# The first feed-forward network by seven products over all tokens, with some weight remainders made by adding DMAs

## The chip, the cores and the metric

The kernel runs on one core of a Trainium2 chip. The metric is the device time of one execution in microseconds (us); less is better. The core's engines work in parallel, each through its own list of instructions in order, and wait for one another by semaphores: PE (TensorE, matrix products; PEld loads its weights), DVE (VectorE), ACT (ScalarE), POOL (GpSimd) and SP (SyncE, which here only issues DMAs). Matrix products write to PSUM, a small memory of eight banks; everything else lies in SBUF.

## The reference

Two layers work on 512 latent tokens (`x`) and 256 context tokens (`ctx`) of width 1024. Each layer has adaLN-modulated norms, an attention block and a SwiGLU feed-forward network (FFN) with 2816 hidden columns. In layer 0 the FFN is computed for both kinds of token, in layer 1 for the latent tokens only.

```python
FFN_HIDDEN = (8 * D_MODEL + 3 * 256 - 1) // (3 * 256) * 256      # 2816
def swiglu(h, w1, w3, w2):
    return (jax.nn.silu(h @ w1) * (h @ w3)) @ w2

for layer in range(DEPTH):                                       # DEPTH = 2
    ctx_out = layer < DEPTH - 1
    ...
    h_x = modulate(rmsnorm(x, norm_g[layer, 1]), mod_x[3], mod_x[4])
    x = x + mod_x[5] * swiglu(h_x, ffn_w1[layer], ffn_w3[layer], ffn_w2[layer])
    if ctx_out:
        ctx = ctx + mod_c[2] * o_c
        h_c = modulate(rmsnorm(ctx, norm_g[layer, 1]), mod_c[3], mod_c[4])
        ctx = ctx + mod_c[5] * swiglu(h_c, ffn_w1[layer], ffn_w3[layer], ffn_w2[layer])
return rmsnorm(x, final_g)
```

## The kernel before

**Numbers.** Every operand of a product is kept as two fp32r parts: `hi`, a rounded copy, and `lo`, what is left of it. A product is three matmuls, hi·hi, hi·lo and lo·hi (`mm3`, L187, L188, L189). `split` (L182, L183) makes the parts: ACT copies to `hi`, DVE subtracts `hi` from the source to make `lo`. For weights loaded by the stream of weights `S`, the same work stands in L154 (ACT) and L155 (DVE). A token operand `h` lies feature-major, in eight tiles of 128 features: `hx[k]` holds both parts of 512 latent tokens, `hc[k]` of 256 context tokens. The residual streams are `xr` and `cr` (`res` in the profile).

**FFN of layer 0** (`ffn`, called once with layer 0; 493 to 1056 us of the profiled execution). The hidden columns are 22 tiles of 128. For each tile, `mm13` computes `w1` and then `w3`: 8 feature tiles of three matmuls of 512 columns for `x` and of 256 columns for the context, into one PSUM tile of two banks. ACT takes the silu of the first (L1058), DVE multiplies by the second (L1065), and `split` makes `g`. Tiles come in groups of two. The down product of a group (`do2`, `mm3` again) is cut into 16 pieces, one for each of 8 output tiles and each kind of token; a piece ends with DVE adding the gated product to the residual (L1125). The pieces of a group are strewn among the products of the next group. PSUM has two pools of two such tiles, used in the order 0, 0, 1, 1.

**What else runs there.** `filler` gives DVE the modulation rows of the remaining adaLN parts: each of the 56 loads of `in_ada_wT_dram` (512 KB) is read twice, by L249 and L250. Two buffers take these loads; a new load is asked for when one has been read. The context's norm (`norm_c`) runs within the first tile: its sum over features is the matmul L289 with a matrix of ones. The order on each engine is set by the scheduler of the language when the kernel is built; it is fixed in the program.

**FFN of layer 1** works by seven products already (Strassen's scheme in Winograd's form): the feature dimension, the hidden columns of a pair of tiles and the tokens are each cut into two halves, and seven products of quarter size (L1486, L1487, L1488; 256 columns, four feature tiles each) take the place of eight. DVE makes the sums of the weights (L448, L449, L451, L452) and puts the products together (L1504, L1505, L1506, L1510, L1512).

Of the kernel before, what the change touches and what calls it, by code (L numbers as in the profile page):

```python
# [15 lines left out]
P = 128  # L16
# [16 lines left out]
def f32(ap):  # L33
    return ap.bitcast(F32)
# [3 lines left out]
def tile_trunk(  # L38
# [145 lines left out]

    def mm3(ps, wh, wl, xh, xl, n=KT):
        for k in range(n):
            nc.tensor.matmul(ps, wh(k), xh(k), start=k == 0, stop=False)  # L187
            nc.tensor.matmul(ps, wh(k), xl(k), start=False, stop=False)  # L188
            end = nc.tensor.matmul(ps, wl(k), xh(k), start=False, stop=k == n - 1)  # L189
        return end  # L190
# [130 lines left out]
    hx, hc = [None] * KT, [None] * KT  # L321

    def h_tiles(*which):
        for k in range(KT):
            if "x" in which:
                hx[k] = hpool.tile([P, 2, NX], F32R, tag=f"hx{k}", name="hx")
            if "c" in which:
                hc[k] = hpool.tile([P, 2, NC], F32R, tag=f"hc{k}", name="hc")
# [77 lines left out]
    groups = [list(range(g, min(g + GRP, HT))) for g in range(0, HT, GRP)]  # L406
    groups = groups[:-2] + [groups[-2], groups[-1]]
    NG = len(groups)

    groups2 = groups[:-2] + [groups[-2] + groups[-1]]  # L410

    def ffn_weights(l):


        def add2(g):
            for j in groups2[g]:
                S.add(w2[l, j * P : (j + 1) * P, :], "w2")

        for g in range(NG):
            for j in groups[g]:  # L420
                for w in (w1, w3):
                    S.add(w[l, j])

                    if 0 < g < NG - 1 and (j, w is w1) == ((groups[g][0], True) if g > 1 else (groups[g][-1], False)):
                        add2(g - 1)
        add2(NG - 2)

# [62 lines left out]

    ada1 = [(l, s_, k) for l, s_ in [(0, 5)] + [(1, z) for z in range(6)] for k in range(KT)]
    ada1_at = [ada1[max(0, 3 * n - 3) : min(3 * n, KT)] if n < 4 else [] for n in range(2 * NG)]
    for i, z in enumerate(ada1[KT:]):
        ada1_at[4 + i * (2 * NG - 8) // (6 * KT)].append(z)
# [9 lines left out]
    with ExitStack() as st:  # L504
# [36 lines left out]
        with ExitStack() as s0:  # L541
# [4 lines left out]
            h_tiles("x", "c")  # L546
# [390 lines left out]
        for u in range(8):  # L937
# [14 lines left out]
            else:  # L952
# [3 lines left out]
                def prep(m):  # L956
                    def f():
                        if m == 0:
                            h_tiles("x", "c")
# [65 lines left out]
        h_tiles("x")  # L1025
        for k in range(KT):
            h_make(k, hx[k], xr[k], r, 0, 1, 0, nmap)
        ffn_weights(0)
# [4 lines left out]
    def ffn_psum(st):  # L1033

        pools = [st.enter_context(tc.tile_pool(name=f"f_ps{i}", bufs=2, space=PSUM, reuse_waits="tile")) for i in range(2)]
        order = [0, 0, 1, 1]

        def tile_():
            order.append(order.pop(0))
            return pools[order[-1]].tile([P, 1024], F32, tag="f", name="f")  # L1040

        return tile_

    def ffn(l, fp, fps, chunks, first, last, filler=None, between=None, done=None):

        nall = sum(c[3] for c in chunks)
        gt = {}
        evac = [None]  # L1050

        def mm13(ps, w, c):
            wh, wl = (wslice(t) for t in w)
            mm3(ps[:, c[5] : c[5] + c[3]], wh, wl, c[0], c[1])

        def silu_of(j, ps):
            s = fp.tile([P, nall], F32, tag="silu", name="silu", bufs=1)
            act = nc.scalar.activation(s, ps[:, 0:nall], AF.Silu)  # L1058
            if j == HT - 1:
                exp_ln_tables(act)  # L1060
            return s

        def g_of(g, j, ps, s):
            t = fp.tile([P, 2, nall], F32R, tag="g", name="g", bufs=2 * GRP)
            nc.vector.tensor_mul(s, ps[:, 0:nall], s)  # L1065
            end = split(t[:, 0, :], t[:, 1, :], s)
            gt[j] = t
            if g == 0:
                evac[0] = end
            if filler and j == groups[g][0]:  # L1070
                with tc.issue_after(end.ins):
                    filler(2 * g + 1)

        def do13(g, pieces=()):

            pieces = list(pieces)
            n = -(-len(pieces) // (2 * len(groups[g]))) if g > 1 else 0
            if filler and evac[0]:
                with tc.issue_after(evac[0].ins):
                    filler(2 * g)  # L1080
            for j in groups[g]:
                if j == 0:
                    pr = [fps() for _ in range(2)]
                    w = [S.next(), S.next(1)]
                    keep_busy(pr[0], 0 if l else 16, before[0])
                    for ci, c in enumerate(first):
                        for i in range(2):
                            mm13(pr[i], w[i], c)
                            if between and i == 0:
                                between(ci)  # L1090
                else:
                    pr = []
                    for _ in range(2):
                        w = S.next()
                        ps = fps()
                        for c in chunks:
                            mm13(ps, w, c)
# [595 lines left out]
```

## Time and profile before

| what | value |
|---|---|
| time, median of 3 executions | 1674.18 us (1671.73 to 1675.25) |
| the profiled execution's own time | 1676.36 us |
| its span (first to last instruction) | 1674.6 us, 1.8 us less |
| mean granted TensorE clock | 0.99 |
| DVE busy in the FFN of layer 0, 593 to 893 us | 68 to 72 of each 100 us |
| DMA of weights `raw<-in_w_dram` | 132 of 512 KB, 3.8 us from issue to landing |

The page of the profile gives busy times by engine and by group of instructions; a group's line holds the line of the code, the engine, the operation, what is written and read, the shape and count, then the busy time in us and the mean of one in ns, and behind the last bar how long the engine stood idle just before these instructions and what ended the wait. Durations overlap on PE: a matmul starts before the one ahead of it has ended.

### The profile page before, as it was taken

The numbers are of one execution on the slowest core, as the hardware profiler recorded it, in microseconds if no ns is written. First come the engines' busy times: TensorE is split into PE (matmuls) and PEld (weight loads), VectorE is DVE, ScalarE is ACT, GpSimd is POOL, SyncE is SP. The second block draws the span as 40 slices with busy tenths as digits, with TensorE's granted clock in tenths as the row PEclk, the third lists the DMA queues.
The fourth block names the chain that finished last, engine by engine and source line by source line (L and its number), as shares of the span: only waits on it lengthen the run. The fifth ranks groups of instructions, "written<-read, shape, count | busy, mean of one in ns | idle before, by whom it ended". The sixth has DMA issues, their size and how long they took to land.

```text
span 1674.6 us, 26226 instructions
## 1 busy us (share of the span) xinstructions
PE 1609.4 (96%) x10436; PEld 1408.9 (84%) x10436; DVE 1175.9 (70%) x1936; ACT 669.5 (40%) x1235; POOL 233.9 (14%) x270
## 2 busy tenths in 40 slices
PE   5999998999999999999999999999999899999996
PEld 3798987877889888888888888878788798989896
DVE  4758698966578666766766344778665797869685
ACT  4445554556253111112111123456755453524343
POOL 2223113454010000000000000155321000000001
PEclk9999999999999999999999999999999899999998
DMA  9422254644126334534434130221011332323321
GB/s 335 110 55 80 82 161 136 186 133 126 51 76 211 118 113 129 161 112 140 135 117 126 39 101 26 75 80 50 14 39 34 119 126 88 113 90 101 114 76 51
DMA packets 56915, 176.97 MB, mean 106 GB/s; under 512 B 6245, under 2 KB 10501, under 8 KB 56793
## 3 DMA queue, kind: packets, MB, share of 16 engines
q1 hardware_dynamic: 53064, 164.40, 32.2%
q0 software_dynamic: 3152, 10.37, 1.9%
q8 instruction: 82, 1.34, 0.3%
q10 hardware_dynamic: 576, 0.52, 0.1%
q14 instruction: 41, 0.33, 0.1%
HBM read 160.45 MB, written 4.86 MB: 99 GB/s over the span
## 4 chain that ended last, share of the span: by engine, by line
PE 65%; DVE 7%; DMA 3%; ACT 2%; issue 1%; POOL 0%; DVEq 0%; SPq 0%; ACTq 0%; POOLq 0%
PE f L187 10%; PE f L188 10%; PE f L189 10%; PE f L1486 4%; PE f L1488 4%; PE f L1487 4%; PE t L1313 3%; DMA raw<-in_w_dram 2%; PE lin L187 2%; PE lin L189 2%; PE lin L188 2%; DVE wl L155 2%; PE f L1540 2%; PE f L1541 2%; PE t L1299 2%; PE f L1539 2%
## 5 line engine op out<-in xcount | busy, mean ns | idle before, releaser
L154 ACT CAST wh<-raw 128x1024 fp32r<-128x1024 f32 x126 | 131.4, 1049 | 469.2 <-PE f L188 326.1
L155 DVE TENSOR_TENSOR wl<-raw,wh 128x1024 fp32r<-128x1024 f32 x126 | 158.2, 1256 | 81.6 <-ACT wh L154 81.4
L187 PE MATMUL f<-hx,wh 128*128 128x512 f32 (+1 forms) x416 | 161.6, 392 | 6.2 <-DVE res L1125 5.3
L188 PE MATMUL f<-hx,wh 128*128 128x512 f32 (+1 forms) x416 | 160.9, 387 | 0.0
L189 PE MATMUL f<-hx,wl 128*128 128x512 f32 (+1 forms) x416 | 160.5, 386 | 0.0
L188 PE MATMUL f<-g,wh 128*128 128x256 f32 (+1 forms) x416 | 137.1, 330 | 0.0
L189 PE MATMUL f<-g,wl 128*128 128x256 f32 (+1 forms) x416 | 136.0, 328 | 0.0
L187 PE MATMUL f<-g,wh 128*128 128x256 f32 (+1 forms) x416 | 135.5, 330 | 0.0
L187 PE MATMUL lin<-hx,wh 128*128 128x512 f32 x264 | 107.9, 409 | 5.6 <-DVE q L354 2.2
L249 DVE SCALAR_TENSOR_TENSOR junk<-raw,tables 128x1024 bf16<-128x1024 f32 x80 | 98.2, 1228 | 17.7 <-DMA raw<-in_ada_wT_dram 17.1
L188 PE MATMUL lin<-hx,wh 128*128 128x512 f32 x264 | 105.7, 400 | 0.0
L1125 DVE SCALAR_TENSOR_TENSOR res<-f,mod,res 128x512 f32<-128x512 f32 (+1 forms) x160 | 92.3, 613 | 18.6 <-PE f L189 18.3
L188 PE MATMUL f<-hc,wh 128*128 128x256 f32 x368 | 104.2, 285 | 0.9 <-DVE hc L337 0.9
L189 PE MATMUL lin<-hx,wl 128*128 128x512 f32 x264 | 105.0, 398 | 0.0
L189 PE MATMUL f<-hc,wl 128*128 128x256 f32 x368 | 103.6, 283 | 0.0
L187 PE MATMUL f<-hc,wh 128*128 128x256 f32 x368 | 102.7, 283 | 0.3 <-ACT hc L336 0.3
L1065 DVE TENSOR_TENSOR silu<-f,silu 128x768 f32<-128x768 f32 x22 | 21.1, 957 | 114.5 <-PE f L189 114.5
L316 POOL TENSOR_TENSOR ns_a<-ns_a,ns_s 128x256 f32<-128x256 f32 (+1 forms) x20 | 19.7, 984 | 584.8 <-ACT ns_s L312 582.9
L187 PEld LDWEIGHTS f<-hx,wh 128*128 128x128 f32 x416 | 78.6, 190 | 22.8 <-DVE res L1125 7.1
L189 PEld LDWEIGHTS f<-hx,wl 128*128 128x128 f32 x416 | 78.6, 189 | 16.2
L188 PEld LDWEIGHTS f<-hx,wh 128*128 128x128 f32 x416 | 78.9, 190 | 14.1
L187 PEld LDWEIGHTS f<-g,wh 128*128 128x128 f32 x416 | 78.5, 190 | 8.0 <-issue 0.2
(326 smaller groups left out, 4636.4 us busy)
## 6 DMA issues: line engine op xcount, KB each, us to landing
raw<-in_w_dram SPq DMA_DIRECT2D x132, 512.0 KB, 3.8
raw<-in_ada_wT_dram SPq DMA_DIRECT2D x80, 512.0 KB, 3.6
raw<-in_w_ab_dram SPq DMA_DIRECT2D x24, 512.0 KB, 4.1
raw<-in_ada_w_dram SPq DMA_DIRECT2D x16, 512.0 KB, 9.4
k<-k SPq DMA_DIRECT2D x16, 384.0 KB, 5.8
raw<-in_w_c_dram SPq DMA_DIRECT2D x12, 512.0 KB, 3.7
nb<-in_na_bias_dram POOLq DMA_DIRECT2D x16, 256.0 KB, 3.7
raw<-in_wo_ab_dram SPq DMA_DIRECT2D x8, 512.0 KB, 3.7
```

The costliest lines, as they stand in the source:

```text
L154: nc.scalar.copy(hi, raw)
L155: eng.tensor_sub(lo, raw, f32(hi))
L187: nc.tensor.matmul(ps, wh(k), xh(k), start=k == 0, stop=False)
L188: nc.tensor.matmul(ps, wh(k), xl(k), start=False, stop=False)
L189: end = nc.tensor.matmul(ps, wl(k), xh(k), start=False, stop=k == n - 1)
L249: nc.vector.scalar_tensor_tensor(junk, raw, 1.0, cs[0], op0=ALU.mult, op1=ALU.mult, accum_out=col[:, 0])
L1125: evac[0] = nc.vector.scalar_tensor_tensor(res(m), ps[:, 0:n], mod[l][:, 5, v, m : m + 1], res(m), op0=ALU.mult, op1=ALU.add)
L1299: nc.tensor.transpose(t[:, k, :], d["p"][c][:, k * P : (k + 1) * P], ident)
L1313: nc.tensor.matmul(o[64 * c : 64 * c + 64, 0:P], v[:, kt, 64 * kv : 64 * kv + 64], pt[:, c, k, :], start=(k == 0), stop=(k == nb - 1),)
L1486: nc.tensor.matmul(ps, wh(k), b[:, 0, :], start=k == 0, stop=False)
L1487: nc.tensor.matmul(ps, wh(k), b[:, 1, :], start=False, stop=False)
L1488: nc.tensor.matmul(ps, wl(k), b[:, 0, :], start=False, stop=k == 3)
```

## The change

**Layer 0's FFN by seven products.** The 22 hidden tiles become 11 pairs. Pairs 0 and 1 stay as they were (`plain_tile`). Pairs 2 to 10 use seven products (`seven`) with latent and context tokens as one block of 768 tokens, cut into two halves of H = 384: a product is 12 matmuls of 384 columns. `hx[k]` and `hc[k]` are slices of one tile `hb[k]`.

**Sums.** `token_sums` makes three combinations of the token halves and splits them into tiles `T`, after hidden tile 2; `first_sum` makes the fourth after hidden tile 3. `pair_weights0` makes the weights' sums in place, with one spare tile.

**Down.** A super-group is one or two pairs (`supers0`). Its down product runs in one piece, within the next super-group's first pair: after tile 2 for pair 0, otherwise between that pair's `w1` and `w3` products. `down` computes two output tiles for both kinds of token into four banks at a time; `to_residual` (L1248) adds them. PSUM is eight tiles of one bank, used in turn.

**Remainders by DMA.** `split_by_dma` makes `lo` with no DVE work for 44 weight pieces: ACT writes the negative source to `lo`, a DMA issued by POOL adds the source, ACT copies the rounded source to `hi`.

**Also:** one buffer instead of two for the adaLN loads (`rows`, reads at L255 and L256); the attention output of layer 1 is split piece by piece into `hb` where it was copied and split whole.

```diff
+    def split_by_dma(hi, lo, src):
+        nc.scalar.activation(lo, src, AF.Copy, scale=-1.0)
+        nc.gpsimd.dma_start(f32(lo), src, accum_op=ALU.add)
+        nc.scalar.copy(hi, src)
...
+    hb = [hpool.tile([P, 2, NT], F32R, name=f"hb{k}") for k in range(KT)]
+    hx, hc = [t[:, :, 0:NX] for t in hb], [t[:, :, NX:NT] for t in hb]
...
+    supers0 = [[0], [1, 2], [3, 4], [5, 6], [7, 8], [9, 10]]
...
+                def ready(n):
+                    if n == 1:
+                        add(spool0[0], a21, a22)
+                    if n == 2:
+                        add(a21, a21, a11)
+                    if n == 3:
+                        add(a11, spool0[0], a11)
+                        add(a12, a11, a12)
+                    return [raw[0], spool0[0], raw[1], raw[0]][n]
...
+            (split_by_dma if first else split)(hi[:, 0:n], lo[:, 0:n], z)
...
-    def ffn(l, fp, fps, chunks, first, last, filler=None, between=None, done=None):
...
-        apool = st.enter_context(tc.tile_pool(name="f_ada", bufs=2, reuse_waits="tile"))
+        apool = st.enter_context(tc.tile_pool(name="f_ada", bufs=1, reuse_waits="tile"))
+        S.pools["parts"] = Turns(wmore, wpool, wpool, wpool)
...
+        fps = lambda: fpp().tile([P, NX], F32, tag="f", name="f")
+        t_tile = lambda: fp.tile([P, 4, 2, H], F32R, tag="T", name="T", bufs=3)
+        q_tile = lambda: fp.tile([P, 4 * H], F32, tag="q", name="q")
...
+        def token_sums():
+            for nm in ("t3", "t4", "t2"):
+                side[nm] = t_tile()
+            for k in range(KT // 2):
+                full = q_tile().rearrange("p (i n) -> p i n", i=2)
+                for i in range(2):
+                    h = hb[k + 4 * i]
+                    nc.vector.tensor_add(full[:, i], f32(h[:, 0, :]), f32(h[:, 1, :]))
+                ...
+                nc.vector.tensor_sub(z["t3"], b22, b12)
+                nc.vector.tensor_sub(z["t4"], b21, b11)
+                nc.vector.tensor_sub(z["t4"], z["t4"], z["t3"])
+                nc.vector.tensor_sub(z["t2"], b11, b12)
+                nc.vector.scalar_tensor_tensor(z["t2"], z["t2"], -1.0, b22, op0=ALU.mult, op1=ALU.subtract)
+                for nm in ("t3", "t4", "t2"):
+                    split(side[nm][:, k, 0, :], side[nm][:, k, 1, :], z[nm])
...
+        def seven(c, first=lambda: None):
...
+            p1, p2 = item("b11", "b21")
+            nc.scalar.copy(u, p1)
+            add(c[0], p2, u)
+            first()
+            (g1,) = item("t1")
+            g3, r4 = item("t3", "t4")
+            g2, r3 = item("t2", "b22")
+            add(u, g2, u)
+            add(c[1], g1, u)
+            for i, z in ((2, u), (3, c[1])):
+                nc.vector.scalar_tensor_tensor(c[i], g3, -1.0, z, op0=ALU.mult, op1=ALU.subtract)
+            add(c[2], r4, c[2])
+            return add(c[1], r3, c[1])
...
+        for n, sg in enumerate(supers0):
+            for p in sg:
+                g = g_tile()
+                late = n and p == sg[0]
+                if p in plain:
+                    for i in range(2):
+                        end = plain_tile(2 * p + i, g, None if p or i else norm_c)
+                        rows(0 if p and i else 3, end)
+                        if late and i == 0:
+                            token_sums()
+                            down(hidden(supers0[n - 1]), (0,))
+                    if p:
+                        first_sum()
+                else:
+                    q = q_tile()
+                    end = seven([q[:, H * i : H * i + H] for i in range(4)])
+                    act = nc.scalar.activation(q, q, AF.Silu)
+                    ...
+                    rows(1, end)
+                    if late:
+                        down(hidden(supers0[n - 1]), (2, 2, 2, 3))
+                    z = z_tile()
+                    ...
```

Three places show how the order on an engine differs. The first is DVE around the first down product. Before the change, the list has at this place the multiplication of a hidden tile (L1065), its split, and the residual additions (`res`) of the first down product:

```order
L252 TENSOR_TENSOR mod_116<-mod_116,adab 128x16 [waits DVE_49]
L155 TENSOR_TENSOR wl<-raw,wh 128x1024 [waits DMAHW2_49,PE_49,Activation_49]
L1065 TENSOR_TENSOR silu<-f,silu 128x768 [waits PE_49,Activation_49]
L155 TENSOR_TENSOR wl<-raw,wh 128x1024 [waits DMAHW4_49,Activation_49]
L1125 SCALAR_TENSOR_TENSOR res<-f,mod_116,res 128x512 [waits DVE_49,PE_49]
L183 TENSOR_TENSOR g<-silu,g 128x768 [waits Activation_49]
L1125 SCALAR_TENSOR_TENSOR res<-f,mod_116,res 128x256 [waits PE_49]
```

After the change, DVE has at the corresponding place, after hidden tile 2 (L1210 is its multiplication, `q` its product), the token sums (L1158 to L1166, and the splits into `T`) and adaLN rows; the middle of this stretch, 44 rows of the same kinds and of two weight sums, is left out:

```order
L1210 TENSOR_TENSOR q<-f,q 128x256 [waits PE_49,Activation_49]
L483 TENSOR_TENSOR res<-raw 128x512 [waits DMAHW5_49]
L485 TENSOR_TENSOR raw<-raw 128x512 [waits DMASW4_49,DMAHW3_49,DMASW1_49,DMAHW7_49,DVE_49,Activation_49]
L183 TENSOR_TENSOR g<-q,g 128x768 [waits Activation_49]
L255 SCALAR_TENSOR_TENSOR junk,mod_116<-raw,tables 128x1024 [waits DMAHW6_49]
L1158 TENSOR_TENSOR q<-hb_124 128x768 [waits DVE_49]
L1158 TENSOR_TENSOR q<-hb_128 128x768
L256 SCALAR_TENSOR_TENSOR junk,mod_116<-raw,csr_4814 128x1024 [waits DVE_49]
...
L1166 SCALAR_TENSOR_TENSOR z<-z,q 128x384 [waits DVE_49]
L1248 SCALAR_TENSOR_TENSOR res<-f,mod_116,res 128x512 [waits DVE_49,PE_49]
L1248 SCALAR_TENSOR_TENSOR res<-f,mod_116,res 128x256 [waits PE_49]
```

So 49 DVE instructions now stand between the split of hidden tile 2 and the first residual addition. The second place is PE at the start of the FFN. Before, the sum of the context's norm (`ones`) stands behind two latent matmuls:

```order
L197 MATMUL f<-ones,ident 128x128 x16
L187 MATMUL f<-hx,wh 128x512 x2
L289 MATMUL f<-ns_a,ones 128x256 x2
L187 MATMUL f<-hx,wh 128x512
L188 MATMUL f<-hx,wh 128x512
```

After, it stands behind all the latent matmuls of the pieces at hand, and the context's own matmuls (256 columns) follow at once:

```order
L194 MATMUL f<-hb_131,wh 128x512
L195 MATMUL f<-hb_131,wl 128x512
L295 MATMUL f<-T,ones 128x256 x2
L193 MATMUL f<-hb_124,wh 128x256 x4
L194 MATMUL f<-hb_124,wh 128x256
```

What moved is the sum: some 70 matmuls later, and right ahead of the products that need the finished norm. The third place is DVE in the steady state of the seven products, here behind a down product (L1248). L1234, L1239 and the like take products out of PSUM, L483 to L488 add weights, L255 and L256 are adaLN rows:

```order
L485 TENSOR_TENSOR raw<-raw 128x512 [waits DMAHW7_49,DVE_49]
L1234 TENSOR_TENSOR z<-f,s 128x384 [waits PE_49,Activation_49]
L255 SCALAR_TENSOR_TENSOR junk,mod_117<-raw,tables 128x1024 [waits DMAHW5_49]
L1318 TENSOR_TENSOR q<-z,q 128x384 [waits DVE_49]
L183 TENSOR_TENSOR wl<-res,wh 128x512 [waits PE_49,Activation_49]
L256 SCALAR_TENSOR_TENSOR junk,mod_117<-raw,csr_4814 128x1024 [waits DVE_49]
L258 TENSOR_TENSOR mod_117<-mod_117,adab 128x16 [waits DVE_49]
L487 TENSOR_TENSOR raw<-res,raw 128x512 [waits DMASW6_49,DMASW1_49]
L488 TENSOR_TENSOR raw<-raw 128x512 [waits DVE_49]
L183 TENSOR_TENSOR wl<-raw,wh 128x1024 [waits PE_49,Activation_49]
L255 SCALAR_TENSOR_TENSOR junk,mod_117<-raw,tables 128x1024 [waits DMAHW7_49]
L1239 TENSOR_TENSOR s<-f,s 128x384 [waits PE_49]
```

All of this is new in layer 0. L487 waits on two of POOL's DMA semaphores (`DMASW`), those of the adding DMAs, since it writes into what they read; L1239, which frees the banks of the next products, stands behind it in the same list.

394 lines of the change are left out of this document (219 added, 175 removed).

## The prediction

> **What bounds the kernel now.** I read the page first: busy times by engine, then the chain of work that ended last.
>
> ```profile
> PE 1609.4 (96%) x10436; PEld 1408.9 (84%) x10436; DVE 1175.9 (70%) x1936; ACT 669.5 (40%) x1235; POOL 233.9 (14%) x270
> PE 65%; DVE 7%; DMA 3%; ACT 2%; issue 1%; POOL 0%; DVEq 0%; SPq 0%; ACTq 0%; POOLq 0%
> PE f L187 10%; PE f L188 10%; PE f L189 10%; PE f L1486 4%; PE f L1488 4%; PE f L1487 4%; PE t L1313 3%; DMA raw<-in_w_dram 2%; PE lin L187 2%; PE lin L189 2%; PE lin L188 2%; DVE wl L155 2%; PE f L1540 2%; PE f L1541 2%; PE t L1299 2%; PE f L1539 2%
> ```
>
> PE bounds it, and L187 to L189 with PSUM tile `f`, three tenths of the span, are the FFN that changes. Then busy times by window (start:end, length, then PE, PEld, DVE, ACT, POOL, each with its count, clock, DMA share, GB/s): two windows of layer 0's FFN, two of layer 1's, which works by seven products already. Behind them the waits, of DVE from 500 to 1000 us and of PE from 490 to 1060 us (total, times, longest).
>
> ```profile
> 793.00:893.00 100.00, 97.94 (x558) 85.77 (x557) 71.77 (x111) 18.64 (x20) 0.00 (x0) 1.00 0.45 134
> 893.00:993.00 100.00, 99.94 (x576) 88.15 (x575) 43.97 (x61) 18.76 (x20) 1.09 (x2) 1.00 0.26 77
> 1410.00:1430.00 20.00, 20.00 (x169) 20.00 (x168) 17.83 (x26) 9.34 (x11) 0.00 (x0) 1.00 0.27 83
> 1430.00:1450.00 20.00, 20.00 (x169) 20.00 (x169) 18.48 (x27) 10.12 (x11) 0.00 (x0) 1.00 0.28 88
> DVE silu L1065 <- PE f L189: 108.3, 18, 7.9
> PE f L187 <- DVE res L1125: 5.3, 7, 1.3
> ```
>
> In layer 0's FFN PE is all but full and DVE waits for PE: fewer PE columns would shorten it. In layer 1's, PE is full with DVE at 18.48 of 20 us, 92%. So seven products can keep PE full, but DVE has little left.
>
> **What is removed on PE.** The window from 893 holds 576 matmuls in 100 us, as many of 512 columns as of 256: a pair takes 347 ns. The window from 1410 holds 169 of 256 columns in 20 us, 118 ns each; one of 512 takes 347 - 118 = 229. One of 384 columns hardly occurs; where it does, its duration lies halfway:
>
> ```profile
> L1275 PE MATMUL s<-gk,gq 128*128 128x384 f32 x64 | 16.5, 339 | 0.0
> L187 PE MATMUL f<-hx,wh 128*128 128x512 f32 x400 | 157.6, 395 | 6.2 <-DVE res L1125 5.3 <-ACT hx L336 0.9
> L189 PE MATMUL f<-hc,wl 128*128 128x256 f32 x368 | 103.6, 283 | 0.0
> ```
>
> (283 + 395) / 2 is 339, so I take 173.5 ns, half a pair. The ends are 118 and 229; that row excludes both. Before: 22 tiles x 2 x 24 = 1056 pairs, 366.4 us. After: 4 plain tiles, 192 pairs, 66.6 us; 9 pairs of tiles x 2 x 7 products x 12 = 1512 matmuls, 262.3 us; together 328.9. **Term 1: -37.5 us.** The down products keep 528 pairs, 183 us. **Term 2: -5.3 us**: the wait for L1125 at seven group starts (row above) goes, since one whole down product runs on banks of its own.
>
> **The context's norm at the start.** Its sum now stands behind some 70 latent matmuls, and the products that need the result follow at once. What lies between, from before's rows: the matmul, a table load, three ACT steps, three to four on DVE, and then the first `h`.
>
> ```profile
> L289 PE MATMUL f<-ns_a,ones 128*128 128x256 f32 x16 | 6.3, 532 | 6.6 <-DVE ns_a L318 6.6
> L269 ACT ACT_TABLE_LOAD x5 | 6.4, 1283 | 0.1
> L295 ACT ACTIVATE ns_y<-ns_t 128x256 f32<-128x256 f32 x7 | 2.9, 418 | 0.2
> L298 DVE SCALAR_TENSOR_TENSOR ns_y<-ns_t,ns_y 128x256 f32<-128x256 f32 x7 | 3.7, 531 | 0.4
> L335 DVE SCALAR_TENSOR_TENSOR ns_h<-res,amod,ns_y 128x256 f32<-128x256 f32 x40 | 20.2, 540 | 0.2
> ```
>
> 0.53 + 1.28 + 3 x 0.42 + 3 x 0.5 + 0.54 + 0.5 is about 5.6 us in which PE has nothing else. **Term 3: +6 us** (0 if work I do not see covers it, 10 with a slowed clock).
>
> **The token sums in DVE's queue.** This is the largest step against the change. By the order, 49 DVE instructions stand between hidden tile 2's split and the first residual addition, L1248. PE reaches the down product right behind tile 2; its third group of four banks reuses the first group's, which L1248 must empty, and everything on PE is queued behind it. The 49 are 8 additions of 768 columns, 30 operations of 384, 8 readings of adaLN rows, two weight sums and a small one:
>
> ```profile
> L183 DVE TENSOR_TENSOR g<-silu,g 128x768 fp32r<-128x768 f32 x22 | 20.9, 950 | 0.0
> L448 DVE TENSOR_TENSOR sum<-raw 128x512 f32<-128x512 f32 x18 | 12.5, 692 | 1.5 <-DMA raw<-in_w_dram 1.2
> L1505 DVE TENSOR_TENSOR q<-f,q 128x256 f32<-128x256 f32 x18 | 7.6, 423 | 0.4
> L249 DVE SCALAR_TENSOR_TENSOR junk<-raw,tables 128x1024 bf16<-128x1024 f32 x80 | 98.2, 1228 | 17.7 <-DMA raw<-in_ada_wT_dram 17.1
> L249 DVE DVE_READ_ACCUMULATOR junk<-raw,tables 128x1 f32 x80 | 6.7, 83 | 0.0
> 569.76 1.22 DVE L155 TENSOR_TENSOR wl<-raw,wh 128x1024 fp32r<-128x1024 f32 x1
> 570.89 1.22 DVE L250 SCALAR_TENSOR_TENSOR junk<-raw,csr 128x1024 bf16<-128x1024 f32 x1
> ```
>
> 384 columns: between 423 and 692, 0.557. So 8 x 0.95 + 30 x 0.557 + 8 x 1.31 + 2 x 0.69 + 0.2 = 36.4 us by durations. The timeline's last two rows start 1.13 us apart at 1.22 each, so a queued operation takes 0.07 to 0.09 less than it lasts: about 33 us. Ahead of it stand 2.3 us (L1210, the `hi` copy, the split). PE meanwhile does two groups, 24 pairs, 8.3 us. 33 + 2.3 + 0.75 (L1248) - 8.3 gives a stall of 28. After a stall the clock falls: behind two waits of 2.9 and 1.0 us, at 1310 and 1313 us, it shows as half (the windows, and PE's waits there):
>
> ```profile
> 1310.00:1316.00 6.00, 4.98 (x17) 4.07 (x18) 2.60 (x7) 2.21 (x5) 0.00 (x0) 0.50 0.01 2
> 1316.00:1319.00 3.00, 3.00 (x13) 2.71 (x12) 2.82 (x8) 1.18 (x3) 0.00 (x0) 0.50 0.00 0
> 1319.00:1322.00 3.00, 3.00 (x20) 2.68 (x20) 2.63 (x7) 2.03 (x5) 0.00 (x0) 0.96 0.01 3
> PE f L289 <- DVE ns_a L318: 2.9, 1, 2.9
> PE f L1486 <- DVE ns_v L294: 1.0, 1, 1.0
> ```
>
> Nine microseconds at half rate lose 4.5; I add 4. **Term 4: +32 us** (25 to 38; 0 only if the residuals were not behind the sums). The Trainium skill (TensorE: Matmul & The Clock Gate, Part 1) has the clock go to half after an idle window of about 3.4 us and come back after about 3.4 us busy. By that the loss would be an estimated 1.7 to 3.4 us in place of 4; this trace's nine microseconds are longer.
>
> **Steady state.** Two pairs take PE 4 x 84 x 0.1735 = 58.3, and their down 96 pairs, 33.3: 91.6 us. DVE's list has for them 32 operations of 384 columns (17.8), 2 of 768 (1.9), 20 of 512 (13.8), 8 of 1024 (9.8), 2 of 1536 (3.6, twice 768 less the start), 24 adaLN readings (31.4) and 16 residuals (9.8; rows just below): 88 us by durations, about 80 as they follow each other. Layer 1 has 92% by durations in its fullest windows; here it is 96% throughout.
>
> ```profile
> L1125 DVE SCALAR_TENSOR_TENSOR res<-f,mod,res 128x512 f32<-128x512 f32 x80 | 59.6, 747 | 16.4 <-PE f L189 16.3
> L1125 DVE SCALAR_TENSOR_TENSOR res<-f,mod,res 128x256 f32<-128x256 f32 x80 | 38.3, 480 | 2.1 <-PE f L189 2.0
> raw<-in_w_dram SPq DMA_DIRECT2D x132, 512.0 KB, 3.8
> k<-k SPq DMA_DIRECT2D x16, 384.0 KB, 5.8
> hx<-hc SPq DMA_DIRECT2D x8, 256.0 KB, 4.5
> L813 POOL DMA_DIRECT2D nb<-in_na_bias_dram x16 | 11.9, 747 | 27.6 <-DVE mx L825 13.1 <-issue 7.1 <-DVE rs L834 4.9
> ```
>
> Walking one period through the order, DVE comes out of the down product's residuals late: the products behind it wait for banks that L1239 empties, 2.5 us a period, and 4 to 5 if L487 also waits for the adding DMA. That DMA is not in this trace. The nearest rows are copies within SBUF, 4.5 us for 256 KB and 5.8 for 384, which extended to 512 KB give 7; it reads two operands, so it may take 12; a plain load takes 3.8. PE needs the pieces about 7 us after issue at three places a period. I take 7: nothing at PE, and 3.5 a period on average, over four periods. **Term 5: +14 us**; from 0 (DVE keeps pace as in layer 1, additions hidden) to 45 (at 9 us, 2 us x 3 places x 4.5 periods more). Of DVE's subtractions, 44 go (1.22 us each); that is in the count above. Issue costs POOL 0.75 each, and POOL has nothing else there.
>
> Attention of layer 1: 32 splits of 128 columns replace 8 of 512 and a copy each; a few us of DVE beside a PE that has other work: 0, give or take 2.
>
> **Sum** against the profiled execution's 1676.4 (span 1674.6, 1.8 around it): 1676.4 - 37.5 - 5.3 + 6 + 32 + 14 = 1685.6. That execution lies 2.2 above the median shown, so **1683 us**, +0.5%.
>
> **The rivals.** *A, the seven products keep pace* and the additions are hidden, term 5 is 0, the token sums cost half to all of term 4: 1669 down to 1653. For it: PE full at DVE 92%. Against: 96%. *B, the token sums do not hold PE*, terms 4 and 5 both 0: 1676.4 - 42.8 + 6 - 2.2 = 1637. It needs residuals ahead of the sums, which the order denies. Both are on the other side of my forecast, faster. *C, late additions*: from 7 us on, PE waits at three places a period; at 9.5, 34 us more: about 1717. *D, descriptors held up*: if POOL could not write a DMA's descriptors while DVE works, each addition would land up to one DVE operation, 1.22 us, later: 1.2 x 13.5 = 16 more, about 1699. The rows speak against it: L813's issue took 747 ns beside a busy DVE. The Trainium skill (SBUF — State Buffer, "SBUF: two separate sides") warns of just this for DMAs from the POOL queue, but for DVE's two-port modes. That the change does not do what it says, I rule out: the order has the 1512 matmuls.
>
> **How the numbers follow.** Chances: forecast (1672 to 1694) 0.45, A 0.25, B 0.07, C 0.15, D 0.08. The range 1650 to 1710 leaves out B and the far half of C. A measurement tells about 0.2%, 3.3 us, from no change: faster (under 1670.8) takes B and A less its top, 0.29; the same to 1677.5, the low end of the forecast and A's top, 0.16; slower 0.55.
>
> **What would show it.** Term 1: 1512 matmuls of 384 columns that follow at about 174 ns. Term 3: one PE wait of 5 to 6 us some 17 us into the FFN. Term 4: one PE wait of about 28 us for L1248, with L1158 to L1166 on DVE meanwhile. Term 5: waits of PE for L1239 or L1242, and DVE's for the adding DMA at L487; the DMA's landing stands in the list of issues. I am wrong if PE is full from the first down product on, or if additions land far from 7 us.

## The result, and the profile after

The changed kernel takes **1725.11 us** (median of 4 executions, 1721.93 to 1726.81), beside 1674.72 us of the kernel before on the same chip: 1.0302 times as long, 95% interval 1.0282 to 1.0322. The prediction had the sign, but it said 1683 us, and its range ends at 1710.

First the page of the changed kernel: busy times, the 40 slices of PE and of its clock (tenths), the chain that ended last, and three of the landings (KB each, us).

```profile
PE 1583.8 (92%) x10220; PEld 1413.8 (82%) x10220; DVE 1255.8 (73%) x2146; ACT 756.1 (44%) x1330; POOL 268.9 (16%) x314
PE   5999989999987499898898999899999899999996
PEclk9999999999999699999999999999999999999999
PE 42%; DVE 11%; DMA 9%; issue 3%; ACT 2%; POOL 0%; DVEq 0%; SPq 0%; ACTq 0%; POOLq 0%
DMA raw<-in_ada_wT_dram 6%; PE f L1618 4%; PE f L1620 4%; PE f L1619 4%; DMA wl<-raw 3%; PE f L1221 2%; PE f L1222 2%; PE f L1223 2%; PE t L1453 2%; DVE junk L255 2%; DVE junk L256 2%; PE f L1672 2%; PE f L1671 2%; PE f L1673 2%; PE t L1439 2%
raw<-in_w_dram SPq DMA_DIRECT2D x132, 512.0 KB, 3.8
raw<-in_ada_wT_dram SPq DMA_DIRECT2D x80, 512.0 KB, 3.6
wl<-raw POOLq DMA_DIRECT2D x42, 512.0 KB, 5.6
```

PE is 25.6 us less busy, as was meant, and the span 45.6 us longer. PE has 42% of the chain in place of 65%; at the head of the chain by lines now stands a DMA, the loads of the adaLN rows, 6%, and DVE's two readings of them have 2% each. Two slices of PE (7 and 4 tenths at 516 to 602 us) show one large hole, and many later slices an 8. The next fence has the main waits of PE and then of DVE from 480 to 1115 us (total, times, longest), which is the changed FFN and the start of layer 1's attention.

```profile
PE f L1254 <- DVE res L1248: 36.5, 4, 34.0
PE f L1221 <- DVE q L1234: 14.7, 4, 4.7
PE f L1221 <- DVE z L1240: 6.7, 4, 2.9
PE f L193 <- ACT hb L337: 5.1, 2, 4.7
PE f L1223 <- DVE wl L183: 3.8, 3, 1.6
PE t L382 <- ACT hb L337: 3.4, 1, 3.4
PE t L194 <- DVE hb L338: 1.1, 1, 1.1
DVE junk L255 <- DMA raw<-in_ada_wT_dram: 64.3, 34, 6.0
DVE res L483 <- DMA raw<-in_w_dram: 25.8, 5, 8.9
DVE raw L487 <- DMA wl<-raw: 5.2, 6, 3.0
```

Before, PE's waits in this FFN came to some 8 us. Now they are 34.0 us at the first down product, 5.1 us for the context's norm, and nearly 30 us in the steady state: products (L1221, L1223) and down products wait for DVE. DVE is not full meanwhile. It stands idle itself: 64.3 us for adaLN loads, 25.8 us for weights.

Measured from PE's first to its last instruction in this FFN (478.5 to 1045.6 us of the span before, 476.3 to 1082.9 after; the 493 to 1056 us given in the description of the kernel before are 10 to 15 us too late), the stage went from 567.1 to 606.6 us. Adding up the start-to-start times of its matmuls gives the parts:

| us | before | after | difference |
|---|---|---|---|
| matmuls at full spacing | 556.9 | 517.5 | -39.4 |
| gaps over 0.25 us | 8.2 | 73.8 | +65.6 |
| the rest (half clock, small gaps) | 2.0 | 15.2 | +13.2 |
| FFN of layer 0 | 567.1 | 606.6 | +39.5 |
| from its end to layer 1's FFN | 252.9 | 262.3 | +9.4 |
| all else | 354.6 | 351.3 | -3.3 |
| span | 1674.6 | 1720.2 | +45.6 |

### The profile page after: what moved, and what is told of

It is laid out like the page before. It is cut to its first block, busy times and chain, and to the rows that moved or that the text cites. A ratio compares the mean times of both kernels' runs of the same rounds, so it can differ in the third digit from the quotient of the medians.

```text
span 1720.2 us, 26350 instructions
## 1 busy us (share of the span) xinstructions
PE 1583.8 (92%) x10220; PEld 1413.8 (82%) x10220; DVE 1255.8 (73%) x2146; ACT 756.1 (44%) x1330; POOL 268.9 (16%) x314
## 4 chain that ended last, share of the span: by engine, by line
PE 42%; DVE 11%; DMA 9%; issue 3%; ACT 2%; POOL 0%; DVEq 0%; SPq 0%; ACTq 0%; POOLq 0%
DMA raw<-in_ada_wT_dram 6%; PE f L1618 4%; PE f L1620 4%; PE f L1619 4%; DMA wl<-raw 3%; PE f L1221 2%; PE f L1222 2%; PE f L1223 2%; PE t L1453 2%; DVE junk L255 2%; DVE junk L256 2%; PE f L1672 2%; PE f L1671 2%; PE f L1673 2%; PE t L1439 2%
## 5 line engine op out<-in xcount | busy, mean ns | idle before, releaser
L182 ACT ACTIVATE wh<-raw 128x1024 fp32r<-128x1024 f32 (+1 forms) x94 | 91.6, 978 | 205.2 <-PE f L1255 63.9
L193 PE MATMUL lin<-hb,wh 128*128 128x512 f32 (+1 forms) x456 | 161.4, 355 | 8.5 <-DVE q L355 2.2
L194 PE MATMUL lin<-hb,wh 128*128 128x512 f32 (+1 forms) x456 | 159.4, 350 | 0.2
L195 PE MATMUL lin<-hb,wl 128*128 128x512 f32 (+1 forms) x456 | 158.3, 347 | 0.0
L255 DVE SCALAR_TENSOR_TENSOR junk<-raw,tables 128x1024 bf16<-128x1024 f32 x80 | 98.2, 1227 | 74.9 <-DMA raw<-in_ada_wT_dram 74.6
L1254 PE MATMUL f<-g,wh 128*128 128x512 f32 (+1 forms) x320 | 108.2, 342 | 36.5 <-DVE res L1248 36.5
L183 DVE TENSOR_TENSOR wl<-raw,wh 128x1024 fp32r<-128x1024 f32 (+1 forms) x94 | 104.7, 1120 | 44.2 <-ACT wh L182 43.5
L1221 PE MATMUL f<-hb,wh 128*128 128x384 f32 x288 | 98.8, 343 | 14.7 <-DVE q L1234 14.7
L1255 PE MATMUL f<-g,wh 128*128 128x512 f32 (+1 forms) x320 | 109.2, 342 | 0.0
L1256 PE MATMUL f<-g,wl 128*128 128x512 f32 (+1 forms) x320 | 107.3, 339 | 0.0
L193 PEld LDWEIGHTS lin<-hb,wh 128*128 128x128 f32 x456 | 86.1, 189 | 22.7 <-issue 3.0
L1618 PE MATMUL f<-hb,wh 128*128 128x256 f32 x360 | 102.3, 285 | 1.0 <-DVE ns_v L300 1.0
L1619 PE MATMUL f<-hb,wh 128*128 128x256 f32 x360 | 102.3, 285 | 0.0
L1620 PE MATMUL f<-hb,wl 128*128 128x256 f32 x360 | 101.8, 285 | 0.0
L1222 PE MATMUL f<-hb,wh 128*128 128x384 f32 x288 | 98.6, 343 | 0.0
L1223 PE MATMUL f<-hb,wl 128*128 128x384 f32 x288 | 98.2, 343 | 0.0
L194 PEld LDWEIGHTS lin<-hb,wh 128*128 128x128 f32 x456 | 86.3, 189 | 11.0 <-issue 0.9
```

Of the source, the lines that this page charges most:

```text
L255: nc.vector.scalar_tensor_tensor(junk, raw, 1.0, cs[0], op0=ALU.mult, op1=ALU.mult, accum_out=col[:, 0])
L1221: nc.tensor.matmul(ps, wh(k), b[:, 0, :], start=k == 0, stop=False)
L1222: nc.tensor.matmul(ps, wh(k), b[:, 1, :], start=False, stop=False)
L1223: nc.tensor.matmul(ps, wl(k), b[:, 0, :], start=False, stop=k == 3)
L1254: nc.tensor.matmul(ps, hi, g[:, 0, cols[v]], start=first, stop=False)
L1255: nc.tensor.matmul(ps, hi, g[:, 1, cols[v]], start=False, stop=False)
```

## The experiments

Three suspects stood after the trace: the first down product (by my theory the token sums ahead of its residuals; or the gate that the residuals multiply by, whose eight adaLN rows arrive through one buffer), DVE's waits in the steady state, and the adding DMAs. All kernels below start from the changed one. The kernel before, run beside each set, was at 1672.3 to 1674.3 us. The last two columns are waits of PE in the profiled execution: for the first residual of the first down product, and all others from 620 us to the end of this FFN added up (the steady state).

| run | edit | median us | ratio to before, 95% | PE: first residual | PE: steady state |
|---|---|---|---|---|---|
| (the change) | | 1725.11 | 1.0302 [1.0282, 1.0322] | 34.0 | 29.1 |
| one_load | one adaLN load instead of 56 | 1662.72 | 0.9949 [0.9932, 0.9965] | 12.6 | 2.4 |
| sums_after | token sums behind the first down product | 1723.97 | 1.0311 [1.0282, 1.0340] | 24.5 | 31.3 |
| one_load_after | both | 1665.68 | 0.9957 [0.9942, 0.9973] | 4.3 | 1.2 |
| no_dma | remainders by DVE, all 44 | 1681.90 | 1.0058 [1.0043, 1.0073] | 30.5 | 3.2 |
| dma_w2 | by DVE: 18 first parts | 1716.07 | 1.0254 [1.0233, 1.0276] | 37.1 | 20.1 |
| dma_first | by DVE: the other 26 | 1700.04 | 1.0164 [1.0149, 1.0179] | 29.3 | 11.4 |
| gate_early | six gate loads ahead, in `T` tiles | 1702.28 | 1.0177 [1.0158, 1.0195] | 4.1 | 28.6 |
| rows_even | adaLN readings spread | 1707.59 | 1.0211 [1.0194, 1.0229] | 33.8 | 18.9 |
| even_gate | gate_early and rows_even | 1685.10 | 1.0071 [1.0054, 1.0087] | 4.3 | 16.4 |
| **even_nodma** | even_gate and no_dma | **1662.94** | 0.9942 [0.9924, 0.9960] | 11.9 | 4.7 |
| gate_nodma_after | gate_early, no_dma, sums_after | 1668.11 | 0.9970 [0.9957, 0.9983] | 5.8 | 1.7 |
| best1 | the same, norms begun sooner | 1670.06 | 0.9975 [0.9964, 0.9986] | 5.9 | 2.0 |
| best2 | best1 and rows_even | 1670.67 | 0.9982 [0.9970, 0.9995] | 6.0 | 4.1 |
| att_whole | attention output split whole | 1720.98 | 1.0283 [1.0265, 1.0300] | 34.0 | 27.9 |

### The loads through one buffer, and the sums

**one_load**: the readings stay, the loads go. All 56 read the data of the first load, so this kernel and one_load_after leave out part of the modulation.

```diff
-                        ada_rows(*ada1[len(ada1) - len(ada1_load) - 1], csr, ada_raw.pop(0), junk)
-                        ada_request(apool)
+                        ada_rows(*ada1[len(ada1) - len(ada1_load) - 1], csr, ada_raw[0], junk)
```

> One adaLN load instead of 56; all 56 readings on DVE stay, each of the first load's data, so layer 1's modulation and layer 0's last gate are not computed rightly. Theory W (DVE stands idle for loads into the single buffer, 64 us in the changed kernel's trace, and so falls behind in the steady state): PE's waits there fall from 32 us to under 8, with the half clock behind them, and the time from 1725 to 1680 to 1690; the wait before the first down product stays near 32, since 36 us of DVE work still stand ahead of it. Rival V (the volume of DVE's work): waits stay over 25 us, time within 8 us of 1725. Rival X (the adding DMAs): the same as V.

**sums_after**: `token_sums` is issued after the last residual addition of the first down product.

```diff
-                            token_sums()
-                            down(hidden(supers0[n - 1]), (0,))
+                            with tc.issue_after(down(hidden(supers0[n - 1]), (0,)).ins):
+                                token_sums()
```

> The token sums are held behind the first down product's last residual addition; nothing else. Theory S (my prediction's term 4: the sums ahead of the first residual hold PE): the wait of 34 us falls to 10 or less, PE then waits some 10 us for the sums at the first seven products, time near 1705. Rival G (the first residual needs the gate, whose eight adaLN rows come through one buffer at 6 to 8 us each, the last at 579 us): the wait only falls to 25 to 30, the sums' delay is added behind, time 1725 to 1740.

**one_load_after** has both.

> Both edits: one adaLN load (modulation not computed rightly) and the sums behind the first down product. If both causes stand in series at the first down product, its wait falls under 8 us only here; PE waits for the sums at the first seven products, 5 to 15 us; time 1655 to 1675. By theory S alone it would show no more than sums_after there.

The waits of PE for the first down product's residual, from 470 to 1110 us: one_load, sums_after, one_load_after, in this order (the residual's line shifts with the edit).

```profile
PE f L1257 <- DVE res L1251: 12.6, 1, 12.6
```
```profile
PE f L1254 <- DVE res L1248: 29.0, 5, 24.5
```
```profile
PE f L1257 <- DVE res L1251: 4.3, 1, 4.3
```

Moving the sums alone leaves 24.5 of 34 us, close to rival G's 25 to 30 and far from theory S's 10, and brings new waits behind, so the time does not move; taking the loads away leaves 12.6; both, 4.3. So the gate is the larger cause, and the sums are the smaller. The timeline of DVE in the changed kernel shows why (start, duration, and in brackets the idle time ahead):

```profile
541.84 1.23 DVE L255 SCALAR_TENSOR_TENSOR junk<-raw,tables 128x1024 bf16<-128x1024 f32 x1 [4.33 <-DMA raw<-in_ada_wT_dram]
...
548.65 1.22 DVE L255 SCALAR_TENSOR_TENSOR junk<-raw,tables 128x1024 bf16<-128x1024 f32 x1 [1.73 <-DMA raw<-in_ada_wT_dram]
549.80 0.08 DVE L255 DVE_READ_ACCUMULATOR junk<-raw,tables 128x1 f32 x1
549.80 1.82 DVE L1158 TENSOR_TENSOR q<-hb 128x768 f32<-128x768 f32 x2
...
573.38 1.23 DVE L255 SCALAR_TENSOR_TENSOR junk<-raw,tables 128x1024 bf16<-128x1024 f32 x1 [0.33 <-DMA raw<-in_ada_wT_dram]
...
579.28 0.17 DVE L258 TENSOR_TENSOR mod<-mod,adab 128x16 f32<-128x16 f32 x1
...
580.77 3.90 DVE L1248 SCALAR_TENSOR_TENSOR res<-f,mod,res 128x512 f32<-128x512 f32 x7
```

L258 completes the gate from eight rows, 518 to 579 us, one every 7 to 10 us; the residual cannot start before it. The token sums lie between the rows. In this trace DVE is busy 32.7 of the 34.1 us that PE waits, so it alone does not tell the loads from the sums. The trace of sums_after does: with the sums out of the way the rows still come only every 6 to 8 us, and DVE stands idle 2.2 to 4.6 us ahead of each for its load. In one_load, where the rows are early, the builder's order puts two of the four rounds of sums behind the first residual and leaves two ahead; one_load_after moves those too.

The steady state answers at once. In one_load PE's waits there are 2.4 us in all, in place of 29.1; below, its waits, and then its busy times over 575 to 985 us (length, PE, PEld, DVE, ACT, POOL, clock, DMA share, GB/s):

```profile
PE f L1224 <- DVE q L1237: 1.3, 2, 1.0
PE f L1224 <- DVE s L1242: 1.1, 3, 0.4
```
```profile
575.00:985.00 410.00, 407.59 (x2343) 388.06 (x2342) 344.00 (x571) 156.50 (x171) 30.80 (x36) 1.00 0.46 112
```

PE is 99% busy with the same 44 adding DMAs and the same DVE work. So theory W held in the steady state. It missed at the first down product, where it had the wait stay near 32 us; that wait shrank too, and so the time is 1663 us and not 1680 to 1690. One thing this run does not tell apart: without the loads DVE need not wait for them, and SP's queue, which also issues the loads of weights, is free of their requests. Both kinds of wait show in the change: in the down product at 664 to 700 us DVE stands idle 9.0 us for four adaLN loads and 8.9 us for one load of weights (L483).

### The adding DMAs

**no_dma**:

```diff
     def split_by_dma(hi, lo, src):
-        nc.scalar.activation(lo, src, AF.Copy, scale=-1.0)
-        nc.gpsimd.dma_start(f32(lo), src, accum_op=ALU.add)
-        nc.scalar.copy(hi, src)
+        split(hi, lo, src)
```

> All 44 remainders that an adding DMA made are made by DVE's subtraction again (1.14 us each in a queue, 50 us more on DVE). Theory W or V: DVE falls further behind, PE's steady waits rise by 10 to 30 us, time 1735 to 1755. Rival X (the additions, 5.6 us to landing, are what is late): waits fall, time under 1715.

Both theories that I had set against X missed: with 44 more operations on DVE the kernel is 43 us *shorter*. X has its time here, though it had failed in one_load, where it had the time stay near 1725. Busy times in the steady state, first of the change (605 to 1045 us), then of no_dma (600 to 1005 us):

```profile
605.00:1045.00 440.00, 410.87 (x2293) 388.26 (x2292) 334.90 (x549) 152.98 (x163) 31.43 (x37) 0.98 0.61 160
```
```profile
600.00:1005.00 405.00, 403.18 (x2321) 385.63 (x2320) 366.95 (x574) 122.28 (x131) 0.00 (x0) 1.00 0.39 126
```

DVE went from 76% to 91% busy, and PE from 93% to nearly 100%. So the volume of DVE's work was not what PE waited for. Its halves:

```diff
# dma_w2
-            (split_by_dma if first else split)(hi[:, 0:n], lo[:, 0:n], z)
+            split(hi[:, 0:n], lo[:, 0:n], z)
# dma_first, in dma_parts and last_parts
-        split_by_dma(hi, lo, raw[0])
+        split(hi, lo, raw[0])
```

> Only the 18 first parts of the pairs' weights are split by DVE again; w2, the first plain weights and the last ones keep the adding DMA (26). Theory R (an adding DMA holds the raw buffer that the weight sums and the next loads need, so L483 and, through SP's queue, the adaLN loads are late): most of no_dma's gain is here, time 1680 to 1695. Rival N (the number of additions, or POOL's queue): about half of the gain, 1700 to 1710.

> The complement: the 18 first parts keep the adding DMA, w2, the first plain weights and the last ones are split by DVE again. Theory R: little gain, 1710 to 1725. Rival N: about half of no_dma's gain, 1700 to 1710.

Neither theory fits both: taking 18 additions away gained 9 us, taking the other 26 away 25, together 34 of 43. Rival N has the time of dma_first (1700) and not that of dma_w2 (1716). Theory R, that the pairs' first parts do the harm, fell. But the order of DVE's list changes with each of these kernels, so they do not say whether the additions or the order cost.

### The gate ahead, the readings spread

**gate_early**: six of the gate's loads go into two of the `T` tiles, which are empty until the token sums; then four readings follow each of tiles 0 and 1.

```diff
+        gate = [f32(t_tile()).rearrange("p a b n -> p (a b n)") for _ in range(2)]
+        for i in range(6):
+            raw = gate[i // 3][:, 1024 * (i % 3) : 1024 * (i % 3) + 1024]
+            nc.sync.dma_start(raw, ada_wT[ada1_load.pop(0)])
+            ada_raw.append(raw)
...
-                        rows(0 if p and i else 3, end)
+                        rows((4, 4, 0, 0)[2 * p + i], end)
```

> The first six of the gate's eight adaLN loads go into two T tiles, which stand empty until the token sums; four readings follow tile 0 and four tile 1. The adding DMAs and everything later are as in the change. Theory G (the first down product waits for the gate, whose rows come through one buffer): its wait falls from 34 us to under 12, the time from 1725 to 1690 to 1700, the steady state's 32 us of waits stay. Rival S (the token sums ahead of it): the wait stays over 25, time over 1715.

The wait for the first residual fell from 34 to 4.1 us (first row below, where two small later waits are in the 6.0), the steady state stayed, and the time fell by 23 us, a little less than expected.

```profile
PE f L1261 <- DVE res L1255: 6.0, 3, 4.1
PE f L1228 <- DVE q L1241: 14.7, 4, 4.7
PE f L1228 <- DVE z L1247: 6.2, 3, 2.9
```

**rows_even** spreads the readings: by the program, the change has nine of a period's twelve with one down product.

```diff
-            add(c[0], p2, u)
+            rows(1, add(c[0], p2, u))
...
-            add(u, g2, u)
+            rows(1, add(u, g2, u))
...
-                    rows(1, end)
...
-                        down(hidden(supers0[n - 1]), (2, 2, 2, 3))
+                        down(hidden(supers0[n - 1]), (1, 1, 1, 1))
...
-                    rows(p % 2 if p < 9 else 0, end)
```

> The change with the readings spread as in even_gate and nothing else: the gate's loads still come through the single buffer, and the adding DMAs stay. If the causes are separate, the wait of 34 us at the first down product stays and the steady waits fall from 32 to under 15 us, time 1700 to 1710. Rival (the gate's delay also feeds the steady state): over 1715.

The time is as expected and the wait of 34 us stays, but the steady waits fall only to 18.9 us, not under 15. In the change's trace the loads are read in runs of eleven, 6 to 9 us apart, with pauses of 13 and 16 us between the runs; here they are read 6 to 10 us apart almost throughout. PE's wait for the first product behind a down product (L1234) was 14.7 us; it and the next, and DVE's wait for the adaLN loads, are now:

```profile
PE f L1221 <- DVE q L1234: 1.2, 2, 0.7
PE f L1221 <- DVE z L1240: 6.5, 3, 3.6
DVE junk L255 <- DMA raw<-in_ada_wT_dram: 77.3, 34, 4.7
```

DVE's wait for these loads has grown, from 64.3 us, and yet PE waits less. So it is not the sum of DVE's waits that holds PE up, but how many of them fall ahead of what PE needs next.

**even_gate** has both edits; **even_nodma** has no_dma in addition, and differs from even_gate in nothing else.

> gate_early, and the adaLN readings spread: one for each quarter of a down product and two within each set of seven products, in place of nine in the down product. The adding DMAs stay. Theory P (readings crowded behind the down product cost one turnaround of the single buffer each, 3.6 us, and DVE falls behind): PE's steady waits of about 30 us fall under 12, time from 1702 to 1675 to 1685. Rival A (the adding DMAs themselves make weights late, however the readings stand): waits stay over 20, time over 1693.

> even_gate with all 44 remainders by DVE: beside even_gate only the adding DMAs differ. Theory P alone (once the readings are spread, additions are hidden, and no_dma gained only because its order spread them): within 4 us of even_gate's 1685. Rival A (additions cost by themselves, through weights that land late and buffers held longer): 1668 to 1676.

even_gate's 1685.1 us is at the end of theory P's range, and its 16.4 us of steady waits lie between P's 12 and A's 20. even_nodma's 1662.9 rules out theory P alone and is below the range of rival A too.

Against the change, rows_even gains 17.5 us, gate_early 22.8, and both together 40.0: two separate causes. Taking the additions away on top gains another 22.2 (1685.1 to 1662.9), with the readings at the same places of the program. So the additions cost as well, in the direction of rival A; but DVE's list, as the builder orders it, is again another one, and what share of the 22 us is order no run shows. The gain lies in the steady state (16.4 to 4.7 us of waits): the first residual waits longer without the additions, 11.9 us in place of 4.3. Over 620 to 1040 us, busy times of even_gate and DVE's waits for the two DMAs, then the same of even_nodma (whose FFN ends at 1026 us, so the last 14 us are attention):

```profile
620.00:1040.00 420.00, 403.32 (x2254) 375.22 (x2253) 323.48 (x531) 149.80 (x159) 34.29 (x39) 0.99 0.61 169
```
```profile
DVE junk L255 <- DMA raw<-in_ada_wT_dram: 57.4, 26, 3.9
DVE raw L487 <- DMA wl<-raw: 13.6, 8, 3.6
```
```profile
620.00:1040.00 420.00, 413.70 (x2360) 389.12 (x2359) 377.38 (x591) 127.56 (x142) 5.55 (x7) 1.00 0.40 128
```
```profile
DVE junk L253 <- DMA raw<-in_ada_wT_dram: 18.0, 24, 2.4
```

DVE is 54 us busier in even_nodma and waits 53 us less for the two DMAs. Three ways from the additions to these waits show. First, an addition takes 6.2 us to land in even_gate (median of 42) and holds its buffer meanwhile; SP's queue, which issues the weight loads and the adaLN loads in one order, stands 46 us there for such a buffer (`SPq L127 <- DMA wl<-raw: 46.1, 13, 8.0`). Second, L487 waits for an addition. Third, the loads themselves land later beside additions: from 620 to 1020 us those of weights in 4.4 us (median) against 3.6 in even_nodma, those of adaLN rows in 7.3 at the longest against 5.1. How the 22 us divide, no run tells. But the additions do not cost by themselves: in one_load all 44 stay, SP's queue stands 88.8 us for their buffers from 600 to 1020 us, and DVE waits for them at L487 about as long as here:

```profile
DVE raw L487 <- DMA wl<-raw: 10.8, 6, 2.5
```

Yet PE's steady waits are 2.4 us there. The price of the additions was seen only beside the adaLN loads.

even_nodma is the fastest of all that compute everything: 0.58% below the kernel before (0.40 to 0.76).

### Two smaller ones, and the rest

**gate_nodma_after** had the gate's loads ahead, no additions, and the sums moved.

> The gate's loads early as in gate_early, all remainders by DVE as in no_dma, the token sums behind the first down product. Theory (the causes add up: gate 34 us, DVE's waits in the steady state 32 us and the half clock behind both): PE's waits in this FFN fall under 15 us, time 1640 to 1655, faster than the kernel before. Rival: what is taken away at the first down product comes back as a wait for the sums at the first seven products, time 1665 to 1680.

The 1668 us lie in the rival's range. What the rival names is only a part of it: the steady waits went, but 5.8 us stayed at the first residual, some 4 came back for the sums, and a wait of 6.5 us came at the FFN's end. **best1** tried to take that one away (`if m == 0: next_norm()` in place of `m == 2`, and `between()` ahead of the first product), **best2** spread its readings.

> gate_nodma_after with the next layer's norm begun after the first context output tile in place of the third, and the context's norm written ahead of the first product. Theory (the wait of 6.5 us for the next layer's h at the FFN's end is a norm begun too late): time 1658 to 1664. Rival (DVE's and ACT's order at the end is set elsewhere): within 3 us of 1668.

> best1 with the adaLN readings spread as in even_gate. By theory P little is left to gain here, since no_dma's order had the readings 6 to 10 us apart already: within 4 us of best1. Rival (its remaining waits are DVE's for the single buffer, 21 us): 5 to 10 us less than best1.

Both are within 3 us of 1668, and the wait at the end is 6.6 us still in best1. The edit of best1 moved nothing: every engine runs the same instructions in the same order as in gate_nodma_after. So theory and rival were not tried, and the 2.0 us between the two medians show how far two sets of executions of one order can lie apart. even_nodma, without the sums moved, is 5 to 8 us below all three by the medians; its interval just touches that of gate_nodma_after.

**att_whole**:

```diff
-                split(*(z[:, i // 2, P * (i % 2) : P * (i % 2) + P] for z in att(m)), o[:, 0:P])
+                nc.scalar.copy(hc[m][:, i // 2, P * (i % 2) : P * (i % 2) + P], o[:, 0:P])
...
+        def prep1(m):
+            return lambda: split(*att(m), f32(hc[m]))
```

> The change with layer 1's attention output copied and split whole as before the change (its remainder is zero, since the copy is rounded already). Theory (my prediction's last term, 0 give or take 2, held, and the 10 us that lie between the two FFNs come from norms that are late at the first FFN's end): time within 4 us of 1725. Rival (the 32 small splits delay that stage): 4 to 8 us less.

4.1 us less, at the edge between the two theories, and the stretch between the two FFNs is 258.7 us in place of 262.3. That points to the small splits for some 4 of its 9.4 us, but it is not shown: the two kernels were run in different sets, their intervals overlap, and a difference of 2 us came up between sets of one order. At the start of the stretch stand waits of PE for norms (L382 and L194 in the list above, 4.5 us), the same in att_whole, with slow clock behind them; that was not tried.

## Why the prediction was wrong, point by point

- **Term 1** (-37.5) was right: -39.4. The 384-column matmuls follow each other at 173 ns; the halfway estimate was 173.5.
- **Term 2** (-5.3) was right: the seven waits for L1125 at group starts are gone. Three short ones for residuals (2.6 us together) came up within later down products; they count with term 5.
- **Term 3** (+6, the context's norm) was right: 5.1 us of waiting (`PE f L193 <- ACT hb L337`), and the clock behind it.
- **Term 4** (+32, 28 of stall) was right in place and nearly in size: 34.0. Its reason was the smaller half of the truth, and the size was luck: with the sums out of the way, in sums_after, PE still waits 24.5 us. I saw 49 instructions ahead of the residual and took the eight readings among them as work; I did not follow the residual's own operand back. It needs the gate, and the gate's rows come one per 7 to 10 us. The forecast's sign hung on this term.
- **The clock behind a stall.** I added 4 us. The trace shows less. Behind the long wait PE ran at half clock for about 4.9 us and then at full, which loses about 2.5 (windows of the changed kernel; the clock is the column after POOL). The figure of the Trainium skill (TensorE: Matmul & The Clock Gate, Part 1), by which I had estimated a loss of 1.7 to 3.4 us, was nearer.

```profile
581.90:586.80 4.90, 4.90 (x16) 4.08 (x16) 4.90 (x11) 0.00 (x0) 0.00 (x0) 0.52 0.00 0
586.90:592.00 5.10, 5.10 (x32) 4.44 (x31) 5.10 (x11) 0.00 (x0) 0.00 (x0) 1.00 0.28 80
```

- **Term 5** (+14, 0 to 45) **is the step that failed**. Waits and slow clock behind the first down product came to about 46 us: of the 73.8 us of gaps, 34.7 are neither the first residual nor the norm, and most of the rest's +13.2 follows them. I priced DVE by volume, 88 of 91.6 us a period, and gave the adaLN readings 1.31 us each. What this put at nothing, without a reason, is the turnaround of their one buffer: from the end of L256 to the next L255 stand 3.4 us at least, and from one L255 to the next 6.0 at least (2.5 in one_load). Nine loads so take 54 us or more of DVE's list, where I had the down product at 33 us; the products behind them came late, 14.7 us of PE's wait for L1234 alone. one_load shows that it was the loads and not the volume (2.4 us of steady waits with the same DVE work), rows_even that their bunching counts, and in no_dma DVE at 91% held PE up by almost nothing. The second part of the step is the additions, next point. Also, the upper end of 45 does not follow from its working: 14 and 2 x 3 x 4.5 are 41.
- **The additions** I took at 7 us, and hidden there. They land in 5.6 (4.5 to 8.7 over the 42), sooner than I took; yet even_nodma without them is 22 us shorter, with the readings spread. Rival C needed landings beyond 7 us at which PE waits for the pieces. PE hardly waited for a landing itself: what the trace shows are buffers held, later loads and DVE's wait at L487, of which I had named only the last, in the 4 to 5 us a period.
- **Rival D**, with the Trainium skill's warning (SBUF — State Buffer, "SBUF: two separate sides"), did not show: POOL's issue of an addition took 863 to 916 ns beside a DVE busy three quarters of the time, and no landing took over 8.7 us. Whether any DVE operation here was in the modes that the warning is about, no run shows.
- **Rival A** had DVE keep pace as in layer 1. Without the bunched loads and the additions it does: even_nodma's PE is 98.5% busy with DVE at 90%, near the 92% of layer 1's fullest windows.
- **The last term** (attention, 0 give or take 2) was 9.4; perhaps 4 of it are the splits it spoke of, and the rest was in no term.

## What to carry to other kernels

An engine that works in order is bounded by its waits as well as its work: give each load through a single buffer its whole turnaround (reading, request, landing) on the reader's time line, and count how many fall into one stretch. Before blaming what stands ahead of a late instruction, follow each of its own operands to where it is made. Moving work from an engine to a DMA pays only if that engine's busy time holds the others up, and a DMA holds buffers and delays loads that the engine may wait for; here it took 44 subtractions from DVE, and even_nodma, which gives them back, is 22 us shorter than even_gate.

## What the runs showed that I had not expected

An adding DMA from SBUF onto SBUF of 512 KB lands in 5.6 us (median of 42, 4.5 to 8.7), about 2 us later than a load from HBM of the same size (3.6 to 3.8 over the whole kernel), and POOL is busy 0.87 us with its issue. Beside such additions the loads of weights in this FFN land in 4.4 us in place of 3.6 (medians of even_gate and even_nodma). PE stayed 98.5 to 99.5% busy with DVE at 90 to 91% over 400 us (even_nodma, no_dma), more than this kernel had shown over so long a stretch before.
